# A longer lag between the broadcast reciprocals and their product in the forgetting attention of a hybrid encoder trunk

## The chip, the core and the metric

The kernel runs on one NeuronCore of a Trainium2 chip (trn2). The metric is the device time of one launch in microseconds; the median of several executions counts. The engines, as the profile names them: PE (TensorE; PEld is its weight loading), DVE (VectorE), ACT (ScalarE), POOL (GpSimd) and SP (SyncE, which here only issues DMAs). Each engine takes its instructions in program order and waits at each one for the semaphores it needs.

## The reference

Two layers, each: RMSNorm of `x` [2048, 1024]; one input projection, whose columns feed three token mixers; a SiLU gate on each; concatenation; output projection; RMSNorm; residual. The mixers are a gMLP gate, retention, and the forgetting attention (FoX) with 6 heads of width 64:

```python
logits = jnp.einsum('bqhd,bkhd->bhqk', qb, kb).astype(jnp.float32) * scale
logits = logits + cum_f[:, :, q0:q1, None] - cum_f[:, :, None, :q1]
logits = jnp.where(causal, logits, -jnp.inf)
p = jax.nn.softmax(logits, axis=-1).astype(v.dtype)
outs.append(jnp.einsum('bhqk,bkhd->bqhd', p, vb))
...
f_out = f_out.reshape(b, s, F_WIDTH) * jax.nn.silu(f_g)
```

The kernel leaves the exponentials unnormalized until the value product is done; then it multiplies the result by the gate and by the reciprocal of each row's sum.

## The kernel before, in words

All matrix products run in float32 with data split into two parts of 12 bits, H and L (`split`, L167): a copy on ScalarE gives H, a subtraction on VectorE or GpSimd gives L. A layer is: the input projection with retention and gMLP behind it (`in_proj`), FoX (`class Fox`, `fox`), and the output projection with the norms (`out_proj`).

FoX goes over the heads h = 0 to 5, in each over the query blocks s = 0 to 3 of 512 tokens, in each over the key tiles j of 128 tokens up to the diagonal (4, 8, 12 and 16). One (h, s, j) is one step, 40 steps a head and 240 a layer. The loop in `fox` (L732) issues for each step, in the order of ORDER (`"ltesv"`):

- l: the L part of the last transposed tile, on VectorE (L670);
- t: four transposes of exponentials on PE (L659) for the value product three steps ahead, and the copy to H on ScalarE (L671). For the key tiles in ON_POOL ScalarE copies the tile to `Ts` instead (L664), and GpSimd makes H (L665) and L (L666): key tile 3 of block 0, 5 of block 1, 4 and 8 of block 2, 4, 8 and 12 of block 3;
- e: an exponential on ScalarE (L646);
- s: up to two score tiles on PE (L612, L613) with mask and running minimum on VectorE (L630), some 19 tiles ahead;
- v: the value product on PE, one product with H and one with L (L688, L689).

Then come at most one load from GpSimd's queue (`ld.issue`, L567: queries `q`, keys and values `kv`, low key rows `kL`; those of the next head are queued when block 0, and for `kL` block 1, of a head is done) and `bg.tick()`, which moves each background generator on by one `yield`.

After the last key tile of a block, step i, `finish` (L694) becomes such a generator. Two steps on it adds the two halves of the accumulator and sums the denominators. For even heads it ends there. For odd heads, twelve times a layer, it takes the pair of heads further: reciprocals, the load of the gate into `gy` (L714); FX steps on the transposition of the reciprocals on PE (L717), their copy (L719) and store to DRAM on SP (L721); RA steps on two loads that broadcast them to 64 partitions each (L724), which wait for that store; RB steps on GpSimd's product of gate and reciprocals (L726); RC steps on GpSimd's product with the attention result (L728); RD steps on the store of the block (L730). With (2, 2, 4, 1, 3) these are the steps i+1, i+3, i+5, i+9, i+10 and i+13.

```python
for i in range(2):
    nc.sync.dma_start(out=rb[i * HD:(i + 1) * HD], in_=scr[4 * i:4 * i + 4].rearrange("r p -> (r p)").partition_broadcast(HD))
yield from wait(RB)
nc.gpsimd.tensor_tensor(out=g, in0=g, in1=rb, op=ALU.mult)
yield from wait(RC)
nc.gpsimd.tensor_tensor(out=rb, in0=o2, in1=g, op=ALU.mult)
yield from wait(RD)
nc.sync.dma_start(out=self.y[s][1][m], in_=rb)
```

The schedule is the program order (`manual_schedule`). Tiles named by `U` and `up.tile` share a pool of NU = 29 slots of 4 KB a partition; a new tile takes a slot whose last user is done. Near the end of FoX the output weights are loaded and split as well (`out_weights`, L760, from OW steps before the end, most of the L parts on GpSimd through L177), and `out_proj` begins OPRE steps before the end. Its token tiles go on ticking the same generators, eight ticks a tile.

Of the kernel before, what the change touches and what calls it, by code (L numbers as in the profile page):

```python
# [15 lines left out]
PSUM = bass.MemoryType.PSUM  # L16
# [8 lines left out]
NSB = 4  # L25
EPS = 1e-6
BIG = 1e30
NU = 29  # 4 KB slots for everything of [128, 1024]
NS = 3  # PSUM banks of the scores
# The pace of the work behind the main stream of matrix products, in its steps.  # L30
LEAD = 19  # FoX: score tiles ahead of the value products
SB = 512  # columns of scores that a second score tile in a step may not pass
PRE = 20  # score tiles during the last chunk of the input projection
EMAX = 2  # exponentials that may wait
TK = (1, 4, 7)  # steps of the last projection tile with a transposed tile
ON_POOL = ((3,), (5,), (4, 8), (4, 8, 12))  # key tiles that GpSimd splits, by query block
ORDER = "ltesv"  # of the parts of a step
FX, RA, RB, RC, RD = 2, 2, 4, 1, 3  # between the parts of a finished head pair
QA = 4  # weight row blocks loaded ahead
OL, OE = 9, 16  # normalized tiles behind the output projection, and the last ones  # L40
OW, OD, OP = 22, 3, 4  # output weights: first step, one not used, one split on VectorE
OPRE = 6  # output projection begun before the end of FoX
WU = 30  # matrix products that bring the tensor engine to its full clock


class Background:
    """Work that follows the main stream of matrix products, some ticks behind."""

    def __init__(self):
        self.active = []  # L50
# [20 lines left out]
def wait(n):  # L71
    for _ in range(n):
        yield
# [3 lines left out]
def trunk(ctx, tc, a, out):  # L77
# [8 lines left out]
    tp = ctx.enter_context(tc.tile_pool(name="tp", bufs=2))  # L86
    up = ctx.enter_context(tc.tile_pool(name="up", bufs=NU))
    ctx.enter_context(tc.manual_schedule())
# [4 lines left out]

    BANKS = {"S": (512, NS), "B": (512, 6 - NS), "D": (512, 2)}

# [69 lines left out]
                yield  # L165

    def split(src, on_pool=False):  # L167
        """The parts H and L of float32 data, H + L exactly the data, each of 12 bits."""
        t = U("HL", F32R)
        n = 1  # L170
        for d in src.shape[1:]:
            n *= d
        H, L = t[:, 0:n], t[:, 512:512 + n]
        v = (lambda ap: ap) if len(src.shape) == 2 else (lambda ap: ap.rearrange("p (k c) -> p k c", c=src.shape[2]))
        nc.scalar.copy(out=v(H), in_=src)  # L175
        eng = nc.gpsimd if on_pool else nc.vector
        eng.tensor_tensor(out=v(L), in0=src, in1=v(H), op=ALU.subtract)  # L177
        return H, L

    def weight_gen(pieces, dst, pool=lambda k: True, ahead=2):  # L180
        """Loads and splits the eight row blocks of a weight chunk, one per step."""
        pend = []
        for k in range(KT + ahead):
            if k < KT:
                if k % 2 == 0:
                    f2 = U("wf")
                f = f2[:, (k % 2) * 512:(k % 2 + 1) * 512]
                off = 0
                for src, w in pieces:
                    ap = src[k]  # L190
                    o_ = f[:, off:off + w]
                    if len(ap.shape) == 3:
                        o_ = o_.rearrange("p (c e) -> p c e", c=ap.shape[1])
                    nc.sync.dma_start(out=o_, in_=ap)
                    off += w
                pend.append(f[:, :off])
            if k >= ahead:
                dst.append(split(pend[k - ahead], on_pool=pool(k)))
            yield
# [5 lines left out]
        return [token_half(hT, t, g) for g in range(2)]  # L205

    def in_proj(l, hT, w0, cur, next_norm):
        """Input projection and everything of it but FoX attention."""
        w_in = a["w_in"][l].rearrange("(k p) e -> k p e", p=P)
        rz = w_in[:, :, 768:2304].rearrange("k p (c e) -> k p c e", c=4)  # L210
        az = w_in[:, :, 0:768].rearrange("k p (c e) -> k p c e", c=3)
        chunks = [("v", [(w_in[:, :, 3072:3456], 384), (w_in[:, :, 3840:3846], 6)]),
                  ("g", [(w_in[:, :, 3456:3840], 384)]),
                  ("q", [(w_in[:, :, 2304:2688], 384)]), ("k", [(w_in[:, :, 2688:3072], 384)])]
# [1 line left out]
        chunks += [(("r", m), [(rz[:, :, :, m * P:(m + 1) * P], 512)]) for m in range(3)]  # L216
        W = [w0] + [[] for _ in chunks[1:]]

        # rows of a head: L, H, ones of the queries; H, L, cumulative forget gates of the keys
        qk = [[dram.tile([2, 2 * HD + 2, SEQ], F32, name=f"qk{l}{w}{m}") for m in range(3)] for w in range(2)]  # L220
        vscr = dram.tile([SEQ, 6, P], F32, name=f"vscr{l}")
        gscr = [dram.tile([P, SEQ], F32, name=f"gscr{l}{m}") for m in range(3)]
# [3 lines left out]
        qbds = tp.tile([P, 2, 2, P], F32, name="qbds", tag="qbds", bufs=1)  # L226
        nc.vector.memset(qbds, 0.0)

        # ---- queries and keys of FoX, transposed: weights stationary, tokens moving
        def qk_post(which, m, b, z):  # L230
            zt = U("zHL", F32R)
            zH, zL = zt[:, 0:512], zt[:, 512:1024]
# [11 lines left out]
        def T_chunks(hs):  # L244
# [5 lines left out]
            for ci in (1, 2, 3):  # L250
                for b in range(4):
                    nxt = []
                    wg = None
                    for m in range(3):
# [4 lines left out]
                        if m == 0 and b == 3:  # L259
                            wg = weight_gen(chunks[ci + 1][1], W[ci + 1], lambda k: k % 3 > 0, QA)  # L260
                            for _ in range(QA):
                                next(wg)
# [17 lines left out]
                    hs = nxt  # L280
            return hs

        # ---- the other chunks: tokens stationary, weights moving
        def v_post(t, z):
            vv = up.tile([P, 6, 2, HD], F32R, name="vv", tag="u")
            zv = heads(z[:, 0:384])
# [184 lines left out]
        for ci in (0, 4, 5, 6, 7, 8):  # L471
# [3 lines left out]
            last = ci == len(chunks) - 1  # L475
            if ci == 4:
                cur = T_chunks(cur)
            for t in range(NT):
# [6 lines left out]
                for k in range(KT):  # L485
                    H, L = cur[k // 4]
# [10 lines left out]
                    if last and k % 4 == 3:  # L497
                        loads.issue()
                    if fx and k % 2 and fx.chunks < PRE and t >= 10:
                        fx.s_step()  # L500
                        loads.issue()
                        fx.e_step()
                    if last and t == NT - 1 and k in TK:
                        fx.l_step()
# [62 lines left out]
                nc.gpsimd.dma_start(out=o, in_=i)  # L567

    class Fox:
        """FoX attention in steps: score steps (one 128 x <=512 tile) run ahead of value steps."""  # L570

        def __init__(self, loads, gscr, y):
            self.ld, self.gscr, self.y = loads, gscr, y
# [74 lines left out]
        def t_step(self):  # L648
# [12 lines left out]
            PH, PL = t[:, 0:512], t[:, 512:1024]  # L661
            if j in ON_POOL[s] and (h, s) != (5, 3):
                Ts = U("Ts")
# [68 lines left out]
    def fox(fx):  # L732
        ld = fx.ld
        for i, (h, s, j) in enumerate(fx.V):
            for op in ORDER:
                if op == "e":
                    fx.e_step()
                    if len(fx.exps) > EMAX:
                        fx.e_step()
                elif op == "l":  # L740
                    fx.l_step()
                elif op == "s":
                    n = 0
                    while n < 2 and fx.si < len(fx.S) and fx.cols < fx.vcols + LEAD * 512 - n * SB:
                        fx.s_step()
# [27 lines left out]
    def out_proj(l, y, W, og, x_src, x_dst, hT, next_w, ahead):  # L773
# [31 lines left out]
                yield from norm(o, pre, hT, t, OL if t < NT - 2 else OE, "B")  # L805

        def last_tile(cur):
            """The last token tile, its first half of columns ahead of the other."""
            t = NT - 1
            x = load_x(x_src(t))  # L810
            o = U("o")
            junk = U("junk")
            ss = small("ss", [P, 2])
            rs = small("rs", [P, 1])
            cs = [slice(g * 512, (g + 1) * 512) for g in range(2)]
            for g in range(2):
                oo = bank("oo", "S")
                for k in range(KT):
                    H, L = cur[k // 4]
                    c = slice((k % 4) * P, (k % 4 + 1) * P)  # L820
                    w = W[2 * k + g]
                    for xx, i, first, last in ((H, 0, True, False), (H, 1, False, False), (L, 0, False, True)):
                        mm(oo, lhsT=xx[:, c], rhs=w[i], start=(k == 0 and first), stop=(k == KT - 1 and last))  # L823
                    bg.tick()
                nc.scalar.activation(out=junk[:, cs[g]], in_=oo, func=AF.Square, accum_out=ss[:, g:g + 1])  # L825
                nc.vector.tensor_tensor(out=o[:, cs[g]], in0=oo, in1=post[:, cs[g]], op=ALU.mult)
            nc.gpsimd.tensor_tensor(out=rs, in0=ss[:, 0:1], in1=ss[:, 1:2], op=ALU.add)  # L827
            nc.gpsimd.tensor_scalar(out=rs, in0=rs, scalar1=1.0 / DM, scalar2=EPS, op0=ALU.mult, op1=ALU.add)  # L828
            nc.gpsimd.tensor_tensor(out=rs, in0=rs, in1=mhalf[:, 0:1], op=ALU.pow)
            for c in cs:  # L830
                nc.vector.scalar_tensor_tensor(out=o[:, c], in0=o[:, c], scalar=rs, in1=x[:, c], op0=ALU.mult, op1=ALU.add)  # L831
                nc.sync.dma_start(out=x_dst(t)[:, c], in_=o[:, c])
# [3 lines left out]
        nys = load_y(1)  # L836
        yield from wait(OPRE - 4)
        post = load_gain(a["post_gain"][l])
# [8 lines left out]
        for t in range(NT):  # L847
# [9 lines left out]
            for k in range(KT):  # L857
                H, L = cur[k // 4]
# [46 lines left out]

    wg = weight_gen(first_w(0), W0, lambda k: k % 3 > 0)
    xq[0] = load_x(x_src(0))
    for _ in range(WU):  # the tensor engine at its full clock when the first tile is ready
        nc.tensor.transpose(bank("warm", "B")[:, 0:P], ident, ident)
    pg = load_gain(a["pre_gain"][0])  # L910
    next(wg)
# [2 lines left out]
    first = norm(xq.pop(0), pg, hT, 0, 1, "B", (slice(0, 512), slice(512, DM)))  # L914
# [17 lines left out]
    for l in range(depth):  # L932
# [3 lines left out]
        for i in fox(fx):  # L936
# [4 lines left out]
            elif i == len(fx.V) - OPRE:  # L941
# [6 lines left out]
                x_src = lambda t, x1=x1: x1[t]  # L948
            if i >= len(fx.V) - OPRE:
                next(op)  # L950
# [41 lines left out]
```

## Time and profile before

| | |
|---|---|
| median of 3 runs | 2594.93 us (2593.69 to 2598.18) |
| profiled execution: span from its first to its last instruction | 2588.5 us (the page gives no other time of it) |
| PE busy | 2522.0 us (97%) |
| VectorE busy | 1663.9 us (64%) |
| ScalarE busy | 1258.1 us (49%) |
| GpSimd busy | 943.0 us (36%) |
| mean granted TensorE clock | 0.991 |

The profile is of one execution; the span runs from the first to the last instruction. FoX of layer 0 lies at about 800 to 1115 us, that of layer 1 at about 2080 to 2400 us. A busy PE is not PE at its peak, since matrix products are pipelined. A wait for several semaphores is put down to the one that came last by the profile; where the engine named had long been done, it was another, often a DMA.

### The profile page before, as it was taken

To read this page: it belongs to the slowest core of one execution; us is meant where nothing else is said; L and a number is where in the kernel's file an instruction comes from. 1 tells how busy PE (TensorE), PEld (TensorE's weight loads), DVE (VectorE), ACT (ScalarE), POOL (GpSimd) and SP (SyncE) were. 2 spreads that over 40 slices of the span, in tenths; PEclk is the share of its full clock that TensorE was granted. 3 is DMA by queue.
4 is the path that set the end of the run, shared out by engine and by line. 5 is a ranking of instruction groups with operands and counts; after the bars stand their busy time and mean duration, and the time that the engine had idled before them with its cause. 6 is when DMAs were issued, how large, how long until landed. Compare 5 with 4: busy or idle time off the path is not lost. (4 is left out here: it accounts for less than half of the span.)

```text
span 2588.5 us, 39556 instructions
## 1 busy us (share of the span) xinstructions
PE 2522.0 (97%) x13112; PEld 2149.4 (83%) x13112; DVE 1663.9 (64%) x4173; ACT 1258.1 (49%) x2967; POOL 943.0 (36%) x1528
## 2 busy tenths in 40 slices
PE   9999999999999999999999999999999999999998
PEld 8888899787888777778898889987878887777887
DVE  5544577666668888854454445666676788878433
ACT  7543433333336788843344444333332478768221
POOL 3111366444443444431120114664344435353200
PEclk9999999999999999999999999999999999989999
DMA  6435411101051556254431354101012415653443
GB/s 212 115 88 121 112 38 37 41 14 37 12 106 39 111 100 130 76 183 134 135 126 69 100 120 101 49 22 38 22 30 42 81 38 128 109 110 97 166 146 114
DMA packets 188428, 229.87 MB, mean 89 GB/s; under 512 B 24640, under 2 KB 130048, under 8 KB 186688
## 3 DMA queue, kind: packets, MB, share of 16 engines
q1 hardware_dynamic: 147712, 176.61, 23.7%
q0 software_dynamic: 40512, 50.74, 10.7%
q8 instruction: 104, 1.70, 0.3%
q14 instruction: 100, 0.82, 0.1%
HBM read 149.20 MB, written 78.09 MB: 88 GB/s over the span
## 5 line engine op out<-in xcount | busy, mean ns | idle before, releaser
L489 PE MATMUL z<-HL 128*128 128x512 f32 (+2 forms) x1536 | 588.5, 383 | 1.8 <-ACT HL L175 1.8
L491 PE MATMUL z<-HL 128*128 128x512 f32 (+2 forms) x1536 | 561.3, 365 | 3.7 <-DVE HL L177 3.6
L490 PE MATMUL z<-HL 128*128 128x512 f32 (+2 forms) x1536 | 559.1, 364 | 0.6 <-POOL HL L177 0.6
L177 DVE TENSOR_TENSOR HL<-hT,HL 128x512 fp32r<-128x512 f32 x576 | 420.7, 779 | 42.1 <-ACT HL L175 33.6
L865 PE MATMUL oo<-HL 128*128 128x512 f32 x1488 | 355.4, 395 | 0.2
L177 POOL TENSOR_TENSOR HL<-wf,HL 128x512 fp32r<-128x512 f32 (+2 forms) x150 | 179.0, 1199 | 451.2 <-ACT HL L175 332.8
L175 ACT CAST HL<-hT 128x512 fp32r<-128x512 f32 x576 | 324.0, 625 | 0.0
L865 PEld LDWEIGHTS oo<-HL 128*128 128x128 f32 x1488 | 273.3, 188 | 57.8 <-DVE HL L177 1.1
L491 PEld LDWEIGHTS z<-HL 128*128 128x128 f32 x1536 | 288.6, 188 | 38.6 <-DVE HL L177 5.3
L489 PEld LDWEIGHTS z<-HL 128*128 128x128 f32 x1536 | 289.7, 189 | 24.6 <-ACT HL L175 3.1
L490 PEld LDWEIGHTS z<-HL 128*128 128x128 f32 x1536 | 290.3, 189 | 22.7 <-POOL HL L177 0.9
L670 DVE TENSOR_TENSOR PHL<-T,PHL 128x512 fp32r<-128x512 f32 (+3 forms) x402 | 241.2, 604 | 16.5 <-ACT PHL L671 15.7
L671 ACT CAST PHL<-T 128x512 fp32r<-128x512 f32 (+3 forms) x402 | 206.0, 519 | 71.0 <-PE T L659 51.7
L267 PE MATMUL z<-HL 128*128 128x512 f32 x576 | 224.4, 390 | 1.0 <-DVE HL L177 1.0
L266 PE MATMUL z<-HL 128*128 128x512 f32 x576 | 224.5, 390 | 0.0
L268 PE MATMUL z<-HL 128*128 128x512 f32 x576 | 224.2, 389 | 0.0
L612 PE MATMUL S<-kv,q 128*128 128x512 f32 (+1 forms) x480 | 214.8, 449 | 2.2 <-DVE mn L630 2.2
L688 PE MATMUL acc<-PHL,kv 128*128 128x512 f32 x480 | 185.2, 386 | 18.6 <-POOL PHL L665 18.6
L348 ACT COPY v<-z 128x128 f32<-128x128 f32 x96 | 25.5, 266 | 353.2 <-DVE w L344 353.0
L689 PE MATMUL acc<-PHL,kv 128*128 128x512 f32 x480 | 180.8, 377 | 6.7 <-POOL PHL L666 5.7
L613 PE MATMUL S<-kL,q 66*128 66x512 f32 (+1 forms) x480 | 178.6, 372 | 0.0
L646 ACT ACTIVATE row<-row,mn 128x1024 f32<-128x1024 f32 (+2 forms) x192 | 158.1, 824 | 35.7 <-DVE mn L630 32.2
(164 smaller groups left out, 4468.8 us busy)
## 6 DMA issues: line engine op xcount, KB each, us to landing
x<-x SPq DMA_DIRECT2D x48, 512.0 KB
qk<-zHL SPq DMA_DIRECT2D x192, 128.0 KB
wf<-w_in SPq DMA_DIRECT2D x96, 192.0 KB
vscr<-vv SPq DMA_DIRECT2D x32, 384.0 KB
wf<-w_in SPq DMA_DIRECT2D x48, 256.0 KB
kv<-qk POOLq DMA_DIRECT2D x24, 512.0 KB, 6.9
kv<-vscr POOLq DMA_DIRECT2D x12, 1024.0 KB, 8.0
q<-qk POOLq DMA_DIRECT2D x48, 256.0 KB, 4.0
```

The costliest lines, as they stand in the source:

```text
L175: nc.scalar.copy(out=v(H), in_=src)
L177: eng.tensor_tensor(out=v(L), in0=src, in1=v(H), op=ALU.subtract)
L266: mm(z, lhsT=wH[:, c], rhs=H, start=(k == 0), stop=False)
L267: mm(z, lhsT=wH[:, c], rhs=L, start=False, stop=False)
L268: mm(z, lhsT=wL[:, c], rhs=H, start=False, stop=(k == KT - 1))
L489: mm(z[:, :n], lhsT=H[:, c], rhs=wH[:, :n], start=(k == 0), stop=False)
L490: mm(z[:, :n], lhsT=H[:, c], rhs=wL[:, :n], start=False, stop=False)
L491: mm(z[:, :n], lhsT=L[:, c], rhs=wH[:, :n], start=False, stop=(k == KT - 1))
L612: mm(S[:, :n], lhsT=Q[0][:, qc], rhs=K[:, kc], start=True, stop=False)
L670: self.low = lambda: nc.vector.tensor_tensor(out=PL[:, c0:], in0=T[:, c0:], in1=PH[:, c0:], op=ALU.subtract)
L671: nc.scalar.copy(out=PH[:, c0:], in_=T[:, c0:])
L865: mm(oo[g], lhsT=x[:, c], rhs=w[g][i], start=(k == 0 and first), stop=(k == KT - 1 and last))
```

## The change

RB goes from 4 to 10. The rest of the diff drops comments and docstrings and leaves the line numbers as they are.

```diff
-FX, RA, RB, RC, RD = 2, 2, 4, 1, 3  # between the parts of a finished head pair
+FX, RA, RB, RC, RD = 2, 2, 10, 1, 3
```

The steps of the parts become i+1, i+3, i+5, i+15, i+16 and i+19.

## Rows read from the trace of the kernel before

**Rows 1.** Windows, both FoX stages: us, busy PE, PEld, DVE, ACT, POOL, clock, DMA, GB/s.

```profile
800.00:1120.00 320.00, 301.67 (x1805) 252.53 (x1804) 268.85 (x726) 257.83 (x565) 147.78 (x181) 0.98 0.49 109
2080.00:2400.00 320.00, 302.59 (x1781) 252.51 (x1780) 268.47 (x724) 254.33 (x557) 144.17 (x178) 0.96 0.47 102
```

**Rows 2.** Waits of PE, whole span: us in total, times, longest.

```profile
PE acc L688 <- POOL PHL L665: 18.6, 8, 3.3
...
PE acc L689 <- POOL PHL L666: 5.7, 8, 0.9
```

**Rows 3.** Groups of GpSimd: busy us, mean ns of one, idle before and its releasers.

```profile
L726 POOL TENSOR_TENSOR gy<-gy 128x512 f32<-128x512 f32 x24 | 31.2, 1298 | 82.6 <-DMA gy<-rd 42.6 <-DVE mn L630 25.5 <-DVE PHL L670 12.9
L728 POOL TENSOR_TENSOR gy<-o,gy 128x512 f32<-128x512 f32 x24 | 30.8, 1284 | 1.0
```

**Rows 4.** Timeline, layer 0, head 1, block 0: start, length, instruction, idle before.

```profile
861.49 0.28 SPq L721 DMA_DIRECT2D rd<-rT  x1
...
870.36 0.58 ACT L664 COPY Ts<-T 128x512 f32<-128x512 f32 x1
...
873.74 1.27 POOL L726 TENSOR_TENSOR gy<-gy 128x512 f32<-128x512 f32 x1 [9.32 <-DMA gy<-rd]
...
875.00 0.61 POOL L665 TENSOR_SCALAR PHL<-Ts 128x512 fp32r<-128x512 f32 x1
...
875.66 0.49 PE L688 MATMUL acc<-PHL,kv 128*128 128x512 f32 x1 [2.02 <-POOL PHL L665]
...
877.01 0.80 PE L689 MATMUL acc<-PHL,kv 128*128 128x512 f32 x1 [0.85 <-POOL PHL L666]
```

**Rows 5.** Timeline, layer 0, head 5, block 0.

```profile
1074.63 0.29 SPq L721 DMA_DIRECT2D rd<-rT  x1
...
1079.37 1.28 POOL L726 TENSOR_TENSOR gy<-gy 128x512 f32<-128x512 f32 x1 [3.66 <-DMA gy<-rd]
```

**Rows 6.** Windows on the seven half-clock stretches, one of each layer, and their sum.

```profile
876.82:880.24 3.42, 3.23 (x10) 2.56 (x11) 0.69 (x2) 0.58 (x1) 2.67 (x5) 0.50 0.44 142
...
2156.82:2163.65 6.83, 6.26 (x18) 4.58 (x19) 1.39 (x3) 1.06 (x2) 5.51 (x6) 0.50 0.36 116
...
sum 37.55, PE 33.92 PEld 25.86 DVE 7.05 ACT 6.59 POOL 27.92; mean PE 4.85 PEld 3.69 DVE 1.01 ACT 0.94 POOL 3.99
```

**Rows 7.** Head 0 of layer 0, block 2: splits of tiles 4 and 8; window.

```profile
822.56 0.62 POOL L665 TENSOR_SCALAR PHL<-Ts 128x512 fp32r<-128x512 f32 x1 [0.68 <-ACT Ts L664]
...
827.37 0.61 POOL L665 TENSOR_SCALAR PHL<-Ts 128x512 fp32r<-128x512 f32 x1 [2.27 <-ACT Ts L664]
...
815.00:828.00 13.00, 13.00 (x83) 11.11 (x81) 12.60 (x37) 10.93 (x21) 5.01 (x8) 1.00 0.17 47
```

**Rows 8.** Timeline, layer 1, head 3, block 3.

```profile
2315.22 0.58 ACT L664 COPY Ts<-T 128x512 f32<-128x512 f32 x1
...
2317.77 1.27 POOL L726 TENSOR_TENSOR gy<-gy 128x512 f32<-128x512 f32 x1 [8.36 <-DMA gy<-rd]
...
2321.62 0.80 PE L688 MATMUL acc<-PHL,kv 128*128 128x512 f32 x1 [3.26 <-POOL PHL L665]
```

**Rows 9.** Layer 0: windows between equal value products, and PE's waits in FoX.

```profile
824.88:875.66 50.78, 48.49 (x299) 40.97 (x298) 46.88 (x129) 44.57 (x99) 19.25 (x27) 1.00 0.58 100
875.66:1035.15 159.49, 149.25 (x894) 125.71 (x894) 134.47 (x369) 127.80 (x282) 77.81 (x96) 0.98 0.55 113
...
PE acc L688 <- POOL PHL L665: 8.9, 4, 2.7
...
PE acc L689 <- POOL PHL L666: 3.4, 4, 0.9
```

**Rows 10.** Timeline of GpSimd at the end of FoX, layer 0.

```profile
1114.45 1.29 POOL L177 TENSOR_TENSOR HL<-wf,HL 128x512 fp32r<-128x512 f32 x1 [1.49 <-ACT HL L175]
```

**Rows 11.** DMA issues: KB each, median us from issue to landing.

```profile
kL<-qk POOLq DMA_DIRECT2D x24, 264.0 KB, 3.7
```

**Rows 12.** Waits of ScalarE in FoX of layer 0 (850 to 1090 us).

```profile
ACT PHL L671 <- POOL PHL L665: 0.4, 1, 0.4
```

## The prediction

> **What bounds the kernel now.** I read first the busy time by stage, to see which engine is the limit where the change acts. In the two attention stages the tensor engine (PE) is busy 302 of 320 us, VectorE 268, GpSimd (POOL) under 150 [rows 1]: PE is the bound, and only what makes PE wait, or run slower, counts. Then who PE waits for. The longest item of the whole kernel is the first value product (L688) waiting for a high part that POOL makes (L665): 18.6 us in 8 waits; with it go 5.7 us in 8 waits of L689 for the low part (L666) [rows 2]. Then why POOL is late there. POOL sat idle in front of L726, the product with the broadcast reciprocals, for 82.6 us in all [rows 3]; the releasers named are one cause, since VectorE had long been done where it is named, and L726 needs only the two loads into `gy`.
>
> The timeline of one such place shows the chain [rows 4]. The store of the transposed reciprocals leaves SP at 861.49; L726 starts at 873.74, when the broadcast loads behind that store have landed, 12.3 us later. POOL takes its instructions in order. Key tile 4 of query block 2 was copied for it by ScalarE from 870.36 to 870.94, but its split L665 stands behind L726 and starts at 875.00, 4 us after it could. PE has no other work in its order and waits 2.02 us for the high and 0.85 us for the low part. The other seven waits are alike: in each layer they stand behind blocks 0 and 3 of heads 1 and 3, where the key and value loads of the next head fill the queues. In head 5, where no such loads run, the same stretch took 4.7 us [rows 5], and PE did not wait.
>
> [...]
>
> **The change part by part.** Only RB moves, from 4 to 10; no instruction comes or goes. Call i the step whose value product closes a block. L726 moves from i+9 to i+15, L728 from i+10 to i+16, the store of L730 from i+13 to i+19; transposition, store and loads (i+3 to i+5) stay. So 24 L726 and 24 L728, 1.3 us each on POOL [rows 3], and 24 stores on SP move by six steps of about 1.2 us (a head's 40 steps take 48.8 us, below).
>
> *Block 0, heads 1 and 3 (four waits).* Six steps take L726 past the second kL load and the splits of key tiles 4 (i+10) and 8 (i+14). Split 4 then starts when its copy ends, 870.94, and ends by 873; PE asks at 875.66 - 2.02 = 873.64. Split 8 follows 4.8 us behind split 4 where nothing disturbs it [rows 7], so POOL reaches L726 near 877.8, and the loads had landed by 873.74. No wait is left, 4 us to spare; the next split is six steps further.
>
> *Block 3, heads 1 and 3 (four waits).* L726 moves past two kL issues and split 4 (i+14), and stands ahead of split 8 (i+18). In the latest of the four, copy 4 ends at 2315.80 and L726 could start at 2317.77 [rows 8]. A split takes 2 us and a kL issue 0.6, so POOL reaches L726 near 2318.4, 0.6 us after the landing; L726 and L728 end near 2321.0, and split 8 is due at 2315.8 + 4.8 = 2320.6. PE asks for it four steps after 2321.62 - 3.26 = 2318.36, that is 4.8 us later, near 2323.2, and the high part takes 0.7. So no wait is left here either, with 1.5 us to spare.
>
> *The gain.* Idle time 18.6 + 5.7 = 24.3 us [rows 2]. In the seven half-clock stretches PE was busy 33.92 us of 37.55 [rows 6]; at full clock that work takes half, 17.0 us less. Sum 41.3 us. A check by other rows: from the same product of head 0 to that of head 1 it is 50.78 us with one wait of 2.02, so 48.76 without; the next three heads took 159.49, which is 13.2 over three such [rows 9]. With the 2.02 before them, and the 0.85 and half of 3.23 behind, layer 0 has 17.7. By its idle time, 8.9 + 3.4, and three clock drops of 1.6 it has 17.1. The two agree.
>
> [...] The rows show 3.63 us of idle time within those stretches, already in the 24.3, so I take 17.0.
>
> *Is anything late next?* Without the wait PE goes on at once, and VectorE loses its pause. In head 0 the same tiles run with no product on POOL and PE has no wait: 13.00 us busy of 13.00, VectorE 12.60 [rows 7]. VectorE keeps up, narrowly.
>
> *SP.* Now block 0's result store stands ahead of block 1's broadcast loads and holds them until POOL is done. It falls behind those loads, which can only help. The last stores go to 18 steps past the end of attention, and the output projection reads the last block more than 60 steps after that: hidden. *Blocks 1 and 2.* The 2.6 us of two products fall between splits two or more steps away, with the loads long landed: zero. *Head 5's end.* Two products of block 2 move behind the weight splits of steps 232 to 237, those of block 3 into the second output tile. POOL waits 1.49 us for ScalarE near there [rows 10], which covers half of the 2.6 us. Lower bound zero; upper bound 2.6 us a layer, 5.2 in all. I take zero, since the same two products stand in front of the same last splits today. *Slots.* `gy` and `o2` stay live six steps longer. Counting allocations and last uses by the code, at most 23 of the 29 slots are live, before and after. Zero.
>
> So 2588.5 - 41.3 = 2547.2 for the span. The median of the runs lies 6.4 above the profiled span; with that 2553.6. A change under 0.2% (5.2 us) could not be told from none.
>
> **The rivals.** *The loads land later* (0.14). Both kL loads of a block 3 chain were issued behind L726; now they leave POOL ahead of it and share the queues with the broadcast loads. If these come 3.7 us later (a kL load's own time to landing [rows 11]), L728 of the latest chain ends near 2324.1, and split 8 makes PE wait 2 us or more, with a clock drop. At most the four block 3 chains, half of the eight, keep their price, 20.7 us: 2574.3. Against: only the slimmest chain is that close. [...]
>
> *The order is not the cause* (0.04): split 4 is late by itself, or VectorE takes PE's wait over, and the time stays at 2595. Against: head 0 has no wait at that tile, and head 5, whose L726 ended before it, neither.
>
> *Slower: slots run short* (0.03). ScalarE's copy L671 for a new split tile takes a slot; were one free only when a delayed result store lands, PE would wait behind it, at up to 24 places. Priced like today's, 41.3 / 8 = 5.2 us, 24 of them less the gain give 2594.9 + 124 - 41 = 2678; it turns the sign from nine waits on. Against: in the attention of layer 0 that copy waits for PE and once, 0.4 us, for POOL [rows 12], never for a store, and the count leaves six slots.
>
> **How the numbers follow.** The forecast has 0.79: 2553.6 us. Low end: had every place the clock price of a layer 1 stretch, 6.26 / 2 = 3.1 us [rows 6], the gain would be 24.3 + 25.0 = 49.3: 2545.6. High end: the first rival at its full price, 2574. Faster: 0.79 + 0.14 = 0.93; same 0.04; slower 0.03.
>
> **What would show it.** Right: POOL no longer idle before L726; L688 waiting for L665 under 1 us in all; one clock level through both attention stages; the distance between heads near 48.8 us; VectorE's durations unchanged. The block 3 step is wrong if L688 waits at key tile 8 of block 2. The forecast is wrong if the heads shorten and the end does not come sooner, or if PE waits for VectorE instead.

## The result and the profile after

The changed kernel takes **2552.53 us** (median of 4 runs, 2551.26 to 2554.30), the kernel before on the same chip 2594.31 (median of 4, 2589.82 to 2598.18). The ratio is 0.9849, 95% interval 0.9834 to 0.9865: 41.8 us less, 1.5%. Forecast were 2553.6 us and a range of 2545.6 to 2574.0.

The page of the changed kernel: the span, the busy time of the engines, the granted clock by slices. Each engine has as many instructions as it had; the span is 38.0 us shorter than the 2588.5 of before.

```profile
span 2550.5 us, 39574 instructions
...
PE 2505.5 (98%) x13112; PEld 2140.4 (84%) x13112; DVE 1665.9 (65%) x4173; ACT 1259.2 (49%) x2967; POOL 944.3 (37%) x1528
...
PEclk9999999999999999999999999999999999999999
```

The busy time by stage, for the answer to [rows 1] (the stage of layer 1 comes sooner, so its window is 40 us earlier), and last a stretch at the end of layer 1's attention. Columns: us, busy time of PE, PEld, DVE, ACT, POOL, granted clock, DMA share, GB/s.

```profile
800.00:1120.00 320.00, 313.12 (x1882) 262.90 (x1881) 279.95 (x737) 262.69 (x578) 154.92 (x191) 1.00 0.51 117
2040.00:2360.00 320.00, 312.74 (x1888) 263.44 (x1887) 285.38 (x783) 265.67 (x589) 153.34 (x197) 1.00 0.48 106
...
2357.60:2361.04 3.44, 3.29 (x8) 2.69 (x9) 2.70 (x7) 1.94 (x5) 3.44 (x3) 0.50 0.91 352
```

PE is now busy 313 us of 320, and the clock reads 1.00 in both stages where it read 0.98 and 0.96. The last row is the one half-clock stretch left there, and it is a new one.

PE's waits (us in total, times, longest). L688 for L665 and L689 for L666, 18.6 and 5.7 us in [rows 2], are no longer among them; the longest item left was never longer than 1.3 us.

```profile
PE T L659 <- DVE PHL L670: 7.4, 13, 1.3
...
PE acc L688 <- ACT PHL L671: 0.9, 2, 0.6
```

The two GpSimd groups of [rows 3] (busy us, mean ns, idle before and its releaser): POOL's idle time in front of L726 went from 82.6 to 0.5 us. The products themselves are longer by 0.06 us each.

```profile
L726 POOL TENSOR_TENSOR gy<-gy 128x512 f32<-128x512 f32 x24 | 32.7, 1364 | 0.5 <-DMA gy<-rd 0.5
L728 POOL TENSOR_TENSOR gy<-o,gy 128x512 f32<-128x512 f32 x24 | 32.2, 1340 | 1.4
```

Timeline of the place that [rows 4] show, layer 0, head 1, block 0 (start, length, instruction, idle before). Splits 4 and 8 are GpSimd's splits (L665, then L666) of key tiles 4 and 8. Split 4 starts 0.09 us after its copy ended, the product that had waited 2.02 us follows with no wait, and L726 comes behind split 8, with no wait 10.7 us after its loads were issued.

```profile
867.71 1.11 SPq L724 DMA_DIRECT2D gy<-rd  x2
...
871.17 0.58 ACT L664 COPY Ts<-T 128x512 f32<-128x512 f32 x1
...
871.84 0.61 POOL L665 TENSOR_SCALAR PHL<-Ts 128x512 fp32r<-128x512 f32 x1 [6.61 <-ACT Ts L664]
...
874.28 0.40 PE L688 MATMUL acc<-PHL,kv 128*128 128x512 f32 x1
...
876.49 0.62 POOL L665 TENSOR_SCALAR PHL<-Ts 128x512 fp32r<-128x512 f32 x1 [2.13 <-ACT Ts L664]
...
878.44 1.28 POOL L726 TENSOR_TENSOR gy<-gy 128x512 f32<-128x512 f32 x1
```

**Where the time went**, by how much sooner the same matrix product starts after the change than before (the order of the products is the same). A place is one of the eight where PE waited, four in each layer. At the start of layer 0's attention the changed kernel is 0.81 us late; past its four places it is 17.82 us early, so they gave 18.6; past the end of that attention 16.50, so 1.3 went back. Layer 1's attention begins 16.50 early; past its four places it is 41.26 early, 24.8 more; past its end 37.59, so 3.7 went back, and so it stays to the end. The eight places gave 43.4 us, the two ends of attention took 5.0, the start 0.8; the last 0.4 of the 38.0 us lie behind the last product.

The larger of the two losses is in these rows, the timeline of the end of attention in layer 1 after the change.

```profile
2346.05 1.29 POOL L728 TENSOR_TENSOR gy<-o,gy 128x512 f32<-128x512 f32 x1
...
2347.37 0.33 SPq L730 DMA_DIRECT2D yT<-gy  x1
...
2347.80 0.87 SPq L767 DMA_DIRECT2D wf<-w_out  x2
...
2353.75 0.62 ACT L175 CAST HL<-wf 128x512 fp32r<-128x512 f32 x1 [1.37 <-DMA wf<-w_out]
...
2354.80 0.44 PE L688 MATMUL acc<-PHL,kv 128*128 128x384 f32 x1 [0.56 <-ACT PHL L671]
...
2357.76 0.48 PE L689 MATMUL acc<-PHL,kv 128*128 128x128 f32 x1 [0.73 <-DVE PHL L670]
```

And the store and the weight load of the same stretch in the kernel before.

```profile
2381.30 0.33 SPq L730 DMA_DIRECT2D yT<-gy  x1
...
2388.02 0.99 SPq L767 DMA_DIRECT2D wf<-w_out  x2
```

Before, the store of head 5's block 1 (L730) left SP 6.7 us ahead of the pair of output weight loads L767. Now POOL ends L728 at 2347.34, the store leaves at 2347.37, and the pair stands behind it: 2347.80, where 41.26 us earlier than before would be 2346.76. ScalarE then waits 1.37 us for weights (L175), its copies L671 for the last value products come later, PE waits three times for under 1 us, and the clock falls for the 3.4 us shown above. PE is busy 3.29 us of these, so the drop costs about 1.6 of the 3.7 us. Whether the store is what starts this is taken up under "The end of head 5".

### The profile page after: what moved, and what is told of

Read it like the earlier page. It is cut to its first block, busy times and chain, and to the rows that moved or that the text cites. A ratio compares the mean times of both kernels' runs of the same rounds, so it can differ in the third digit from the quotient of the medians.

```text
span 2550.5 us, 39574 instructions
## 1 busy us (share of the span) xinstructions
PE 2505.5 (98%) x13112; PEld 2140.4 (84%) x13112; DVE 1665.9 (65%) x4173; ACT 1259.2 (49%) x2967; POOL 944.3 (37%) x1528
## 3 DMA queue, kind: packets, MB, share of 16 engines
q0 software_dynamic: 40512, 50.74, 10.7%
## 5 line engine op out<-in xcount | busy, mean ns | idle before, releaser
L175 ACT CAST HL<-hT 128x512 fp32r<-128x512 f32 x576 | 324.2, 626 | 0.0
L670 DVE TENSOR_TENSOR PHL<-T,PHL 128x512 fp32r<-128x512 f32 (+3 forms) x402 | 241.4, 604 | 18.2 <-ACT PHL L671 17.4
L671 ACT CAST PHL<-T 128x512 fp32r<-128x512 f32 (+3 forms) x402 | 206.4, 520 | 58.4 <-PE T L659 43.9
L688 PE MATMUL acc<-PHL,kv 128*128 128x512 f32 x480 | 181.3, 378 | 0.9 <-ACT PHL L671 0.9
L689 PE MATMUL acc<-PHL,kv 128*128 128x512 f32 x480 | 176.9, 369 | 1.4 <-DVE PHL L670 1.2
```

The costliest lines, as they stand in the source:

```text
L670: self.low = lambda: nc.vector.tensor_tensor(out=PL[:, c0:], in0=T[:, c0:], in1=PH[:, c0:], op=ALU.subtract)
L671: nc.scalar.copy(out=PH[:, c0:], in_=T[:, c0:])
```

## The experiments

All but two (e4, e5) start from the changed kernel. The kernel before took 2591.4 to 2593.9 us (medians of 9 runs) beside them. Where there is one run alone, only differences far above the scatter are read from it: all 31 runs of the kernel before lie within 15 us, the four of the changed one within 3.

| label | edit | us | span |
|---|---|---|---|
| e1_head5_lag4 | head 5 back to 4 steps | 2548.30 (5 runs) | 2544.5 |
| e2_lag5 | 5 steps | 2569.58 (1 run) | 2567.8 |
| e3_lag9 | 9 steps | 2551.98 (1 run) | 2550.2 |
| e4_lag4_no_loads | 4 steps, no broadcast loads | 2545.04 (1 run) | 2543.2 |
| e5_on_vector | 4 steps, product on VectorE | 2610.37 (1 run) | 2608.6 |
| e6_head5_block1_lag4 | head 5, block 1 back to 4 | 2550.46 (4 runs) | 2547.2 |
| e7_head5_block2_lag4 | head 5, block 2 back to 4 | 2552.20 (5 runs) | 2547.9 |
| e8_lag8 | 8 steps | 2571.29 (1 run) | 2569.5 |
| e9_only_blocks_0_3 | 10 steps for blocks 0 and 3 of heads 0 to 4 only | 2548.97 (5 runs) | 2549.5 |
| e10_lag8_late_kL | 8 steps, kL loads three steps later | 2571.03 (1 run) | 2569.3 |
| e11_lag16 | 16 steps | 2549.08 (1 run) | 2547.3 |

### Is it the place in POOL's order? 5 steps, 9 steps

```diff
-FX, RA, RB, RC, RD = 2, 2, 10, 1, 3
+FX, RA, RB, RC, RD = 2, 2, 5, 1, 3
```

> RB is 5. Theory, order counts: one step puts L726 behind the split of key tile 4 after block 0, but not after block 3. So the four L688 waits of block 0 go, the four of block 3 stay at 2.3 to 3.3 us each; time near 2574. Rival, the time until the loads land counts: 1.2 us more of lag shortens all eight waits by about half, none goes; time near 2580 to 2590.

PE's waits with 5 steps:

```profile
PE acc L688 <- POOL PHL L665: 9.9, 4, 3.3
...
PE acc L689 <- POOL PHL L666: 2.9, 5, 0.9
```

and POOL in layer 0, head 1, block 0:

```profile
870.48 0.61 POOL L665 TENSOR_SCALAR PHL<-Ts 128x512 fp32r<-128x512 f32 x1 [6.60 <-ACT Ts L664]
...
873.01 1.30 POOL L726 TENSOR_TENSOR gy<-gy 128x512 f32<-128x512 f32 x1
```

One step puts L726 behind split 4 in block 0, and these four waits are gone; block 3's four are where they were, since there split 4 comes four steps later in the order. A lag one step longer gives half of the gain (2588.5 - 2567.8 = 20.7 us of span); the length of the lag as such would give a sixth.

```diff
-FX, RA, RB, RC, RD = 2, 2, 10, 1, 3
+FX, RA, RB, RC, RD = 2, 2, 9, 1, 3
```

> RB is 9. Theory, order counts: five steps put L726 behind the split of key tile 4 after block 3 too, so all eight L688 waits go and the time is that of lag 10, 2552 within 3 us. Rival, time counts: the loads of block 3 have not landed by then, the split of key tile 8 is late and four waits of 1 to 2 us stay, 2560 or more.

No wait of L688 for L665 is left, and POOL's idle time in front of L726 is 0.9 us: with 9 steps block 3 is free too. The time of this run lies among those of 10 steps.

```profile
L726 POOL TENSOR_TENSOR gy<-gy 128x512 f32<-128x512 f32 x24 | 31.8, 1326 | 0.9 <-DMA gy<-rd 0.9
```

### 8 steps: the last lag that leaves block 3 behind its wait

```diff
-FX, RA, RB, RC, RD = 2, 2, 10, 1, 3
+FX, RA, RB, RC, RD = 2, 2, 8, 1, 3
```

> RB is 8. Order counts: after block 3 L726 is still ahead of the split of key tile 4, L728 is behind it. So the four block 0 waits are away and the four block 3 waits shrink by one product, 1.3 us, to 1 to 2 us each, with a clock drop behind some of them; time 2556 to 2570. Rival, the time until the landing counts: four steps more than before, 4.9 us, are longer than any wait of 3.3 us, so all are gone and it is 2552.

PE's waits, and then layer 0, head 1, block 3:

```profile
PE acc L688 <- POOL PHL L665: 9.2, 4, 3.0
...
PE acc L689 <- POOL PHL L666: 3.1, 4, 0.9
```

```profile
913.43 0.55 POOL L567 DMA_DIRECT2D kL<-qk  x1
...
915.52 1.09 SPq L724 DMA_DIRECT2D gy<-rd  x2
...
922.73 1.27 POOL L726 TENSOR_TENSOR gy<-gy 128x512 f32<-128x512 f32 x1 [8.75 <-DMA gy<-rd]
...
923.98 0.61 POOL L665 TENSOR_SCALAR PHL<-Ts 128x512 fp32r<-128x512 f32 x1
```

The four waits stay, against the rival's 2552. So between 8 and 9 steps, one change of place in POOL's order, lie 2569.5 - 2550.2 = 19.3 us of span. But the time is 1.3 us above the expected 2556 to 2570, and the waits should have shrunk by L728's 1.3 us each, which no longer stands in front of split 4. They went from 2.65 each (10.6 of before's 18.6 us are block 3's, in 4) to 2.3. The reason, tried next, is the first rival's: the kL load now leaves POOL ahead of the broadcast loads, and these take 922.73 - 915.52 = 7.2 us from their issue to L726 (7.2, 7.2 and 8.6 at the other three places). Before, with that load behind L726, it was 5.9 here (5.1, 5.7 and 6.5 at the others):

```profile
919.85 1.09 SPq L724 DMA_DIRECT2D gy<-rd  x2
...
925.75 1.29 POOL L726 TENSOR_TENSOR gy<-gy 128x512 f32<-128x512 f32 x1 [7.80 <-DMA gy<-rd]
```

### The same with the kL load kept out of the way

```diff
-            if s == 1 and j == 7:
+            if s == 2 and j == 2:
                 ld.c(h + 1)
```

> RB is 8, and the kL loads of the next head are queued seven steps later, behind the split of key tile 4. At lag 8 the waits of block 3 had shrunk from 10.6 to 9.2 us only, where one product of 1.3 us for each should have come off. Theory: the first kL load leaves ahead of L726 there and makes the broadcast loads land 1.2 us later. Then here L726 starts about 6 us after its loads are issued in place of 7.2 to 7.4, the four L688 waits sum to 4 to 6 us, and the time is 2558 to 2567. Rival, kL has no part in it: L726 starts 7 us or more after the issue, the waits stay near 9 us and the time near 2571.

By the code the loads move by three steps of the head, from step 11 to step 14, and not by the seven that the expectation names. PE's waits, and the same place:

```profile
PE S L613 <- DMA kL<-qk: 10.7, 8, 2.5
...
PE acc L689 <- POOL PHL L666: 3.5, 4, 0.9
PE acc L688 <- POOL PHL L665: 2.3, 3, 1.5
```

```profile
916.81 1.09 SPq L724 DMA_DIRECT2D gy<-rd  x2
...
922.49 1.29 POOL L726 TENSOR_TENSOR gy<-gy 128x512 f32<-128x512 f32 x1 [7.58 <-DMA gy<-rd]
```

The broadcast loads take 5.7 us again (5.6 to 6.4 at the other three places), and L688's waits fall from 9.2 to 2.3 us. So the kL load does delay them, place by place by 0.9 to 2.8 us, 1.7 on average, which is what the four waits lost. The time did not fall to the expected 2558 to 2567: the kL loads are now late for PE themselves, 10.7 us, and 2571.03 is 2571.29 within the scatter.

### The wait taken away without moving anything

This one starts from the kernel before; it leaves out the division by the row sums.

```diff
-            for i in range(2):
-                nc.sync.dma_start(out=rb[i * HD:(i + 1) * HD], in_=scr[4 * i:4 * i + 4].rearrange("r p -> (r p)").partition_broadcast(HD))
...
-            nc.gpsimd.tensor_tensor(out=g, in0=g, in1=rb, op=ALU.mult)
+            nc.gpsimd.tensor_tensor(out=g, in0=g, in1=g, op=ALU.mult)
```

> Lag 4 as before the change, but the two broadcast loads are left out and L726 multiplies the gate by itself, so it waits for no late load; the output lacks the division by the row sums. Theory, the wait for the loads is the cause: all eight L688 waits go, time 2552 within 4 us. Rival, the 2.6 us of the two products ahead of the splits are enough to make the tensor engine wait: waits of L688 of 1 us or more stay at most of the eight places, 2565 or more.

The group of the product (this kernel's line numbers are two lower, so L724 is its L726):

```profile
L724 POOL TENSOR_TENSOR gy<-gy 128x512 f32<-128x512 f32 x24 | 26.1, 1088 | 0.3
```

All eight waits are gone with the product still 4 steps behind, and nothing is lost at the ends of attention; the time is 3 us under the low end of the expected 2548 to 2556. So the product itself in front of split 4 (1.09 us here) costs nothing, and in block 3 not even with L728's 1.3 us beside it; the wait for the loads was the price. The edit also takes the loads off the DMA queues, so it does not part the wait from what the loads do to other transfers.

### The wait moved to another engine's queue

Again from the kernel before.

```diff
-            nc.gpsimd.tensor_tensor(out=g, in0=g, in1=rb, op=ALU.mult)
+            nc.vector.tensor_tensor(out=g, in0=g, in1=rb, op=ALU.mult)
```

> Lag 4, but L726 runs on VectorE in place of GpSimd. Theory, a wait costs by what is queued behind it in its engine's order: the wait for the loads now holds VectorE, which the tensor engine needs in every step (minimum of each score tile, low part of each transposed tile), so the wait is felt at more than eight places and costs more: slower than the kernel before, by 20 to 100 us, with the tensor engine waiting for L630 and L670 after the loads. Rival, the product is only too heavy for GpSimd: on the faster engine the waits shrink and the time is between 2552 and 2594.

The group of the product, PE's waits, and one place:

```profile
L726 DVE TENSOR_TENSOR gy<-gy 128x512 f32<-128x512 f32 x24 | 18.2, 759 | 50.0 <-DMA gy<-rd 49.5 <-issue 0.5
```

```profile
PE T L659 <- DVE PHL L670: 35.0, 18, 7.0
PE rT L717 <- DVE rd L711: 17.9, 4, 4.9
```

```profile
873.88 0.69 DVE L726 TENSOR_TENSOR gy<-gy 128x512 f32<-128x512 f32 x1 [4.29 <-DMA gy<-rd]
...
875.75 0.38 PE L717 MATMUL rT<-ident,rd 128*8 128x128 f32 x1 [4.07 <-DVE rd L711]
```

The product itself is shorter (0.76 us for 1.30) and no longer on POOL, yet the kernel is 18 us slower: VectorE waits 49.5 us for the same loads, and behind it stands what PE needs next. Before, the waits of L659 for L670 were 7.1 us, and L711 was not among what PE waited for. The expectation's low end, 20 us, was a little high. On both engines the wait held what stood behind it: in [rows 4] POOL sat idle 9.32 us in front of L726, and split 4, whose copy had ended at 870.94, began at 875.00; here VectorE sat idle 4.29 us in front of L726, and L711, for which PE waited 4.07 us, came behind it at 875.50.

### Far behind: 16 steps

```diff
-FX, RA, RB, RC, RD = 2, 2, 10, 1, 3
+FX, RA, RB, RC, RD = 2, 2, 16, 1, 3
```

> RB is 16. Tests the slots: the gate tile stays live six steps longer still. Theory: no place is short of slots, the order of the eight places stays good, so the time is 2552 within 4 us, what differs lying at the end of attention. Rival, slots run short: ScalarE's L671 or L664 waits for a result store at many of the 24 places and the time is 2560 or more.

ScalarE's copy L671 waits for PE and twice, 2.0 us, for POOL, never for a store: the slots do not run short even here. The time of this run, 2549.08, lies under all four of 10 steps (2551.26 and more) and among those of e1, the next experiment.

### The end of head 5

```diff
-            yield from wait(RB)
+            yield from wait(RB if h < 5 else 4)
```

> Lag 10 for heads 1 and 3, lag 4 for head 5 as before the change. Theory: the changed kernel gives back about 1.3 us at the end of attention in layer 0 and 3 us in layer 1, because block 1's result store of head 5 now stands ahead of output weight loads on SP and waits there for a backlog of GpSimd; ScalarE then waits for the weights and the tensor engine for ScalarE. Then this kernel is faster than the changed one by 2 to 5 us, near 2549, the two waits of L688 for ScalarE's L671 are gone and the eight waits of heads 1 and 3 stay away. Rival: the loss at the end is chance (the granted clock, DMA), then it is 2552 within 1 us.

The median is 4.2 us under the changed kernel's, its highest run (2549.32) under the lowest of the changed kernel (2551.26), the ratio to the kernel before 0.9829 (0.9812 to 0.9846). In the profile, which is of its quickest run, the ends of attention lose 0.1 and 0.3 us instead of 1.3 and 3.7. The timeline at the end of layer 1:

```profile
2337.44 0.33 SPq L730 DMA_DIRECT2D yT<-gy  x1
...
2343.93 1.00 SPq L767 DMA_DIRECT2D wf<-w_out  x2
```

The store is 6.5 us ahead of the pair of weight loads again, and these leave 44.1 us earlier than before, as all else there does (43.8).

Which of head 5's products is it? Each of the next two takes back one block.

```diff
-            yield from wait(RB)
+            yield from wait(4 if (h, s) == (5, 1) else RB)
```

> Lag 10, but 4 for block 1 of head 5. Theory of the loss at the end: it is block 1's store that holds the output weight loads on SP; then this kernel is near 2548 to 2549, like lag 4 for the whole of head 5, and ScalarE waits for the output weights no longer than 1.5 us a layer. Rival, block 2's two products between the weight splits cost it: then it stays near 2552.

```diff
-            yield from wait(RB)
+            yield from wait(4 if (h, s) == (5, 2) else RB)
```

> Lag 10, but 4 for block 2 of head 5. Theory (block 1's store): the loss at the end stays, near 2552, with L688 waiting for ScalarE as at lag 10. Rival (block 2's products): near 2548 to 2549.

The ratios are 0.9834 (0.9814 to 0.9854) and 0.9838 (0.9817 to 0.9859); the ends of attention lose 1.1 + 1.7 and 1.1 + 2.1 us in the two profiles. Neither block by itself brings e1's time: e6 misses the 2548 to 2549 that the theory of block 1's store gave, and e7, near 2552 as that theory has it, has runs from 2548.15 to 2553.32. The two cannot be told apart by time, and the share of each stays open.

```diff
-            yield from wait(RB)
+            yield from wait(RB if h < 5 and s in (0, 3) else 4)
```

> Lag 10 for blocks 0 and 3 of heads 1 and 3 alone, 4 everywhere else. Theory, only these eight places a kernel paid: the time is that of head 5 at lag 4, 2548.3 within 1.5 us, with no L688 wait for L665. Rival, the move of blocks 1 and 2 of heads 1 and 3 gave or cost something too: 2546 or less, or 2551 or more.

0.9826 (0.9811 to 0.9841), 2548.97 us: as e1, so moving blocks 1 and 2 of the other heads is worth nothing that can be measured. The profile of e9 (its slowest run, 2.3 us over the median) loses 0.7 + 2.5 us at the ends of attention although head 5 is as before, in waits of PE for VectorE's L670. So the ends scatter by some 3 us by themselves (e1 loses 0.4 there with the same order); what the moved products add is better read from the medians, 3.6 to 4.2 us, than from one profile. These runs were on different chips, and the intervals of the ratios overlap.

The traces of e6 and e9 also bear on the store. In both, block 1's store leaves well ahead of the pair L767 again (6.8 and 6.6 us). Yet the pair leaves only 40.9 and 39.9 us earlier than before, where the products of head 5 begin 42.6 and 41.1 us earlier: 1.7 and 1.2 us late. In e7, where the store does hold it, the pair is 1.0 us late, as in the changed kernel. So it comes as late without the store in front of it. Only L688's wait for L671 marks the changed kernel (0.56 us in layer 1) and e7 (0.49) and is gone in e6, e9 and e1.

## Why the prediction was right, and the step that failed

**What bounds it, and the cause: right.** The wait for the broadcast loads, in front of key tile 4's split in POOL's order, held PE. The place in the order decides (4, 5, 8 and 9 steps), and the wait for the loads makes the price (e4, e5). The rival that the order is not the cause falls.

**Block 0: right.** POOL reached L726 at 878.44, forecast near 877.8. **Block 3: no wait, as forecast, but with nothing to spare.** The timeline of layer 0, head 1, block 3 after the change:

```profile
913.76 0.55 POOL L567 DMA_DIRECT2D kL<-qk  x1
...
915.64 1.09 SPq L724 DMA_DIRECT2D gy<-rd  x2
...
920.32 0.61 POOL L665 TENSOR_SCALAR PHL<-Ts 128x512 fp32r<-128x512 f32 x1 [6.02 <-ACT Ts L664]
...
923.13 1.29 POOL L726 TENSOR_TENSOR gy<-gy 128x512 f32<-128x512 f32 x1 [0.29 <-DMA gy<-rd]
...
925.76 0.61 POOL L665 TENSOR_SCALAR PHL<-Ts 128x512 fp32r<-128x512 f32 x1
...
926.46 1.30 POOL L666 TENSOR_TENSOR PHL<-Ts,PHL 128x512 fp32r<-128x512 f32 x1
...
927.35 0.40 PE L688 MATMUL acc<-PHL,kv 128*128 128x512 f32 x1
...
927.81 0.50 PE L689 MATMUL acc<-PHL,kv 128*128 128x512 f32 x1
```

The loads took 923.13 - 915.64 = 7.5 us where they took 5.9 before, so POOL waited 0.29 us for them and split 8 came 0.6 us after it was due (920.32 + 4.81, [rows 7]). PE takes the high part at 927.35, 1.0 us after it is done. But the low part (L666) ends at 927.75 and L689 starts at 927.81: the 1.5 us to spare of the forecast counted the high part's 0.7 us and left out the low part's 1.3. In the profiles of e1, e7 and e9 L689 does wait there, 0.2 to 0.6 us at two of the four places. What the first rival feared is real: beside a kL load the broadcast loads come later, by 1.7 us on average (e8 against e10) where it assumed 3.7, and the slack just took it. That the two share queues is not shown: on the page of before GpSimd's loads are the 50.74 MB of q0, and SP's transfers are in q1; how the one delays the other stays open. (Its "2 us or more" of waiting is 1.6 us for the high part by its own figures, 2324.1 + 0.7 - 2323.2.)

**The gain: right, 2.1 us small.** Forecast 41.3, measured 43.4; in the seven other profiles without the eight waits the places gave 41.5 to 44.1, all against the one profile of before. Heads are now 874.28 - 825.72 = 48.56 us apart, forecast 48.8, so the check by heads was nearly exact. The rest, 0.26 us a place, is partly the restart after a wait: the first product took 0.49 us in [rows 4] and takes 0.40 now, and at the one place without a half-clock stretch 3.23 us were gained where the two waits were 2.69. I did not settle it further. The 17.0 us of the sum count on the half-clock stretches going with the waits: they did, the clock reads 1.00 in both stages after the change, where 0.98 and 0.96 were read before.

**Anything late next, SP, blocks 1 and 2, slots: right.** VectorE's 402 instructions of L670 take 604 ns each, before and after; PE's waits for them are 7.4 us (7.1 before), none over 1.3. Blocks 1 and 2 are worth nothing that can be measured (e9), and the slots suffice even at 16 steps (e11).

**Head 5's end: wrong.** "Lower bound zero; upper bound 2.6 us a layer, 5.2 in all. I take zero, since the same two products stand in front of the same last splits today." It measured 1.3 + 3.7 = 5.0 us in the profile and about 4 by the medians, and layer 1 alone passed the bound of 2.6. The step that failed is this term, put at nothing because the order on POOL in front of the last splits stays: PE waits there all the same, and the clock drop behind the waits, some 1.6 us, was in no bound. The step also did not look at SP's queue, where the store that waits for POOL now stands right ahead of output weight loads. That head 5's lag makes the loss is likely: all ten runs of e1 and e9, with head 5 at 4 steps, lie under the four of the changed kernel, and in the profiles the two ends lose none to 3.3 us at 4 or 5 steps (e4, e1, e2, e5, e9), 2.2 to 5.2 at 8 to 16 (e10, e11, e8, the changed kernel, e3). It is not shown, since these runs were on different chips and the intervals of the ratios overlap. By which way it comes stays open: e6 takes the store out of the way, and the pair of loads is late all the same.

**From span to median: 4.4 us too large.** The forecast carried over the 6.4 us between the profiled span of before and its median; for the changed kernel it is 2552.53 - 2550.5 = 2.0. Every run with both figures on record took 1.7 to 1.9 us more than its own span, so the profiled run of before took about 2590.3 (an estimate from these), one of its quick ones: its runs scatter by 15 us (2584.8 to 2600.0), those of the changed kernel by 3. Most of the 6.4 was this scatter, not the launch. So 2552.5 against 2553.6 is partly luck: +2.1 of gain, -5.0 at the ends and -0.8 at the start (which lies between 0.8 late and 0.6 early over all traces) leave the last product 3.7 us and the span 3.3 us later than forecast, and the 4.4 cancels it.

## What to carry to other kernels

In these runs an instruction that waited for a DMA cost by what stood behind it in its engine's queue: on POOL the eight waits cost 43.4 us, and on VectorE, for the same loads, the kernel was another 18 us slower. So put such an instruction behind the next piece of work that the bounding engine needs: here it counted past which instruction it came, and little by how many steps (20.7 us of span with 5, 19.0 with 8, 38.3 with 9, 38.0 with 10). When the last pass of a loop lags too, try the old lag for that pass: here that was about 4 us quicker by the medians, though the reason is not settled. When a split has two parts, reckon the time to spare for the later one. Where the kernel before scatters more than the change is likely to, do not carry its distance from profiled run to median over.

## What the runs showed that I had not expected

The same waits do not always cost the same clock. In the profile of before, one of eight waits brought no half-clock stretch, three brought 3.4 us (layer 0) and four 6.8 (layer 1). With the product on VectorE the clock was 0.96 in layer 0's attention, where it was 0.98, and 0.988 over the whole run for 0.991: as an estimate from these, all eight places had 6.8. This fits the 15 us of scatter that the waits' kernel has and the changed one has not. The record bears it out: over the 27 runs of before that stood beside the experiments the time follows the mean granted clock (correlation -0.91), from 2584.8 us at 0.994 to 2599.0 and 2600.0 at 0.987. As an estimate, 0.007 of the clock over 2590 us is 18 us.

One kL load of 264 KB, issued some 2 us earlier, kept GpSimd waiting longer for two broadcast loads of 128 KB each: from their issue to the product it was 5.1 to 6.5 us without it (before and e10, four places each) and 7.2 to 8.6 with it (e8).
